# Bidirectional RWKV scan: the group norm's output in its input's memory with four buffers, and inverse blocks placed at the end of a step

## The chip, the cores and the metric

One core of a Trainium2 chip. The metric is the device time of one execution in microseconds, here the median of three runs. Engines are named as in the profile: PE is the matrix engine (PEld its weight loads), DVE the vector engine, ACT the scalar engine, POOL the GpSimd engine, SP the engine whose queue issues nearly all transfers. Every engine works through its own list of instructions in order; an instruction that waits holds up all that stand behind it on that engine.

## The reference, cut to what matters

One trunk layer: SwiGLU, a token mixer, SwiGLU. The change is in the mixer, in the scan over 1152 tokens (128 of context, 1024 latent), in both directions, 16 heads of 64, and in the group norm of what the scan gives:

```python
def _rwkv7_step(S, inp):
    r, w, k, v, kk, a = inp
    sa = jnp.einsum('dbhvk,dbhk->dbhv', S, kk)
    S = S * w[..., None, :] - sa[..., :, None] * (kk * a)[..., None, :] + v[..., :, None] * k[..., None, :]
    return S, jnp.einsum('dbhvk,dbhk->dbhv', S, r)
...
    s_final, y = lax.scan(_rwkv7_step, s0.astype(f32), xs)
    y = _from_scan(y)
    mu = jnp.mean(y, -1, keepdims=True)
    var = jnp.mean(jnp.square(y - mu), -1, keepdims=True)
    y = ((y - mu) * lax.rsqrt(var + GN_EPS)).reshape(b, t, D_A) * p['lnx_g'] + p['lnx_b']
    bonus = jnp.sum(r_h * k_h * p['r_k'], -1, keepdims=True) * v_h
    y = (y + bonus.reshape(b, t, D_A)) * g
```

## The kernel before

The scan runs in chunks of 64 tokens. Two halves of the heads (hb 0 and 1, eight heads each) take 18 steps each, so there are 36 steps; a step handles one chunk of the forward and one of the backward direction, side by side in partitions 0 to 63 and 64 to 127. The order of all five engines is written out by hand in this stage (the `manual_schedule` of L1236); what the next stage issues on ACT, DVE, POOL and SP may be mixed in by a scheduler near the end.

**A step** is `main` (L1085). PE multiplies the states into `xy` (L1104, L1110); ACT copies half of it to `Xs` (L1114); then comes slot 0. PE multiplies `Xs` with the inverse block `W` into `us` (L1120), ACT copies it negated to `vu` (L1123); then comes slot 1. PE forms `sp` (L1130), DVE adds it to the state `Sc` (L1131, L1132), PE finishes `xy` (L1136), ACT copies the outputs to `yt` (L1140). After that the transposes `KBT` (PE L1081, ACT L1083) and, at the end of the step, slot 2. PE's L1081 needs a PSUM buffer that DVE's L1131 has to have read. The three slots are calls of `slot_work` (L1217), each followed by matrix products of the gates as a filler of PE (lines 937 to 941; their weights pass ACT L149 and POOL L150).

**The inverse blocks.** `Solve` (L749) inverts the 64x64 triangles of four steps at once while the four steps before run. Its work is cut into pieces numbered n, and n = 3 x (step - 4 i + 8) + slot, so n % 3 is the slot: loads of `Gq` (n = 0, eight transfers on SP), load of `Wd` (n = 1), `pairs` on DVE (L776, L778; n = 2 to 11), `swap` (two transposes on DVE, L786 and L787; n = 12, slot 0), `back` (four loads of `Nt`, L795), `place` (L802: ACT copies the 32x32 inverses into `Wb`, once for each direction), and `ph1`, `ph2` (L811, L818: 64 small products on PE and two ACT copies each). Four steps have one `swap`: steps 0, 4, 8 and so on.

**The group norm** (L1157) is a generator that advances by one slot at a `yield`. It starts in slot 0, at most one per step; there are 18 of them, and five end after the scan, in a loop (L1268) that advances those left and issues ten filler products each time. A norm loads one direction of `y` from memory (L1163, buffers `y0`, three of them) and takes the other from an SBUF buffer (`y1`) or a second copy; POOL adds them (L1170); DVE takes the mean (L1173), POOL subtracts it (L1176), ACT squares (L1178), DVE sums (L1181), POOL takes the power (L1183) and multiplies (L1185); PE transposes (L1193); ACT scales into `yo` (L1197); POOL adds the bonus term `bb` (L1199); SP stores `yo` to `yn` (L951). `bb` and `yo` have one buffer each:

```python
            yo = gn.tile([P, 4, P], F32, name="yo", tag="yo")
            for k in range(4):
                kt = 4 * hb + k
                A.activation(yo[:, k, :], pt[:, k, :], AF.Identity, bias=pcol("lnx_b", kt), scale=pcol("lnx_g", kt))
            yield
            G.tensor_tensor(yo, yo, bb, ALU.add)
            later(yn_d[hb][tt // 3][:, :, sl], yo)
```

`later` puts a store off to the beginning of the next slot (`flush`). The stage that follows loads `yn` and multiplies it with the projections (L1290 on; its products are lines 158 to 160).

Of the kernel before, what the change touches and what calls it, by code (L numbers as in the profile page):

```python
# [9 lines left out]
F32 = mybir.dt.float32  # L10
# [7 lines left out]
P = 128  # L18
# [43 lines left out]
def tile_step(ctx: ExitStack, tc: tile.TileContext, I: dict, O: dict):  # L62
# [414 lines left out]
    with pool("facc") as facc, pool("f1w", side="right") as wmore, pool("f1p", 6, psum=True) as psum, pool("f1a", 2, psum=True) as paux:  # L477
# [6 lines left out]
        with pool("st") as sp:  # L484
# [36 lines left out]
            with tc.manual_schedule(engines={PE.engine, S.engine}):  # L521
                for kt in range(KT + 1):
                    if kt < KT:
                        mods01(kt)
                    if kt:
                        k = kt - 1
# [70 lines left out]
    with pool("mp", 4, psum=True) as psum, pool("ma", 2, psum=True) as paux, \  # L597
# [151 lines left out]
        class Solve:  # L749
# [75 lines left out]
            def at(self, n):  # L825
                if n == 0:
                    self.loads()
                elif n == 1:
                    self.init()
                elif n < 12:  # L830
                    self.pairs((2, 1, 5)[n % 3])
                elif n == 12:
                    self.swap()
                elif n == 13:
                    self.back()
                    self.place(0)
                elif n == 15:
                    self.place(1)
                elif n == 17:
                    self.ph1(0)  # L840
                elif n == 18:
                    self.ph2(0)
                elif n == 20:
                    self.ph1(1)
                elif n == 21:
                    self.ph2(1)
# [26 lines left out]
        with pool("m2") as pl:  # L873
            sols = [Solve(i) for i in range(9)]
            for k in range(22):
                sols[0].at(k)
# [149 lines left out]
    with pool("s1") as pl, pool("gn") as gn, pool("spa", 2, psum=True) as psA, pool("spx", 1, psum=True) as psX, \  # L1026
# [58 lines left out]
        def main(s):  # L1085
# [52 lines left out]
            for d in range(2):  # L1138
                y0, y1 = YR[d]
                A.copy(eh(yt[y0:y1, m[d]]), xy[y0:y1, :, d])  # L1140
                if s % 2 == 1 and other(cs[d] // 2, d) <= s % 18:
                    yy = direct[hb, cs[d] // 2, d] = gn.tile([P, 8, 64], F32, name="y", tag=f"y{1 if cs[d] > 1 else d}", bufs=3)
                    for k in range(2):
                        later(yy[64 * k:64 * k + 64], yt[y0:y1, k])
                elif s % 2 == 1:
                    later(y_d[d][hb][cs[d] // 2].rearrange("(k t) c -> t k c", k=2), yt[y0:y1].rearrange("p k h v -> p k (h v)"))
# [10 lines left out]
        def group_norm(hb, tt):  # L1157
            y0 = y1 = None
            for d in range(2):
                y = direct.pop((hb, tt, d), None)  # L1160
                if y is None:
                    y0 = gn.tile([P, 8, 64], F32, name="y", tag="y0", bufs=3)
                    S.dma_start(y0, y_d[d][hb][tt].rearrange("t (h v) -> t h v", h=8))  # L1163
                elif y1 is None:
                    y1 = y
                else:
                    y0 = y
            yield
            yield
# [22 lines left out]
            for k in range(4):  # L1192
                PE.transpose(pt[:, k, :], y0[:, 2 * k:2 * k + 2, :].rearrange("p h v -> p (h v)"), ident)  # L1193
            yo = gn.tile([P, 4, P], F32, name="yo", tag="yo")
            for k in range(4):
# [259 lines left out]
```

## Time and profile before

| | |
|---|---|
| median of three runs | 3393.1 us (3387.86 to 3394.22) |
| the profiled execution | 3397.27 us, its span 3395.5 us |
| PE busy | 3209.4 us (95%), 25742 products |
| DVE, ACT, POOL busy | 2007.4, 1185.9, 1306.5 us |
| chain that ended last, by engine | PE 64%, DVE 15%, DMA 8%, issue 5%, POOL 4%, ACT 3% |
| TensorE clock granted, mean | 0.965 |
| scan, from the first L1104 to the last step's end | 1662.9 to about 2253.7 us |

The table says that PE is busy nearly all the time; whether a wait elsewhere costs anything is read from the idle time of PE and from the clock it was granted in that stretch, not from the shares of the other engines. A clock of 1.00 is 2.4 GHz, 0.50 is 1.2 GHz; a stretch with a value between has some of each. The stretch of the scan is where the change lies.

### The profile page before, as it was taken

The numbers are of one execution on the slowest core, as the hardware profiler recorded it, in microseconds if no ns is written. First come the engines' busy times: TensorE is split into PE (matmuls) and PEld (weight loads), VectorE is DVE, ScalarE is ACT, GpSimd is POOL, SyncE is SP. The second block draws the span as 40 slices with busy tenths as digits, with TensorE's granted clock in tenths as the row PEclk, the third lists the DMA queues.
The fourth block names the chain that finished last, engine by engine and source line by source line (L and its number), as shares of the span: only waits on it lengthen the run. The fifth ranks groups of instructions, "written<-read, shape, count | busy, mean of one in ns | idle before, by whom it ended". The sixth has DMA issues, their size and how long they took to land.

```text
span 3395.5 us, 62626 instructions
## 1 busy us (share of the span) xinstructions
PE 3209.4 (95%) x25742; PEld 3049.6 (90%) x25742; DVE 2007.4 (59%) x3300; ACT 1185.9 (35%) x2006; POOL 1306.5 (38%) x1026
## 2 busy tenths in 40 slices
PE   7999999999999999878999889989999999999997
PEld 7999999999897887668888778878999999999996
DVE  6888633346637787875677767545674322223467
ACT  4111111124534454452355555544453111111133
POOL 5111211125546666664321442277762111111144
PEclk9999999999999999879999999989999999999998
DMA  6444211123454555457456566557541111111142
GB/s 235 129 131 144 92 50 38 38 75 131 147 210 146 157 164 162 149 162 238 126 162 188 156 197 213 149 172 238 177 147 38 50 39 40 49 38 48 52 134 97
DMA packets 271534, 433.30 MB, mean 128 GB/s; under 512 B 77840, under 2 KB 173584, under 8 KB 270224
## 3 DMA queue, kind: packets, MB, share of 16 engines
q1 hardware_dynamic: 267792, 424.58, 38.8%
q8 instruction: 202, 3.31, 0.4%
q10 hardware_dynamic: 3456, 4.72, 0.4%
q14 instruction: 84, 0.69, 0.1%
HBM read 311.29 MB, written 96.53 MB: 120 GB/s over the span
## 4 chain that ended last, share of the span: by engine, by line
PE 64%; DVE 15%; DMA 8%; issue 5%; POOL 4%; ACT 3%; SPq 1%; DVEq 0%; POOLq 0%; ACTq 0%
PE pg L159 8%; PE pg L160 8%; PE pg L158 8%; PE po L159 5%; PE po L158 5%; PE po L160 5%; PE pm L158 4%; PE pm L159 4%; PE pm L160 3%; DMA fm<-in_w_mod 2%; DVE fm L403 2%; PE pa L1073 2%; PE xy L1104 2%; DVE wl L127 1%; PE ph L808 1%
## 5 line engine op out<-in xcount | busy, mean ns | idle before, releaser
L125 ACT CAST wh<-wr 128x1024 fp32r<-128x1024 f32 x270 | 280.4, 1048 | 808.7 <-PE po L159 430.2
L127 POOL TENSOR_TENSOR wl<-wr,wh 128x1024 fp32r<-128x1024 f32 x117 | 288.7, 2468 | 496.5 <-ACT wh L125 493.6
L295 POOL TENSOR_TENSOR gl<-sg,gh 128x384 fp32r<-128x384 f32 x132 | 157.8, 1195 | 782.8 <-ACT gh L294 782.8
L159 PE MATMUL pg<-h1l,wh 128*128 128x384 f32 x1056 | 356.9, 338 | 6.8 <-POOL h1l L167 6.8
L158 PE MATMUL po<-gh,wh 128*128 128x384 f32 x1056 | 356.5, 338 | 5.0 <-ACT gh L294 3.0
L159 PE MATMUL po<-gl,wh 128*128 128x384 f32 x1056 | 357.6, 339 | 3.6 <-POOL gl L295 3.6
L158 PE MATMUL pg<-h1h,wh 128*128 128x384 f32 x1056 | 358.1, 339 | 0.0
L160 PE MATMUL pg<-h1h,wl 128*128 128x384 f32 x1056 | 356.1, 337 | 0.0
L160 PE MATMUL po<-gh,wl 128*128 128x384 f32 x1056 | 355.6, 337 | 0.0
L158 PE MATMUL pg<-h3h,wh 128*128 128x384 f32 x1056 | 353.7, 336 | 0.0
L160 PE MATMUL pg<-h3h,wl 128*128 128x384 f32 x1056 | 353.3, 335 | 0.0
L159 PE MATMUL pg<-h3l,wh 128*128 128x384 f32 x1056 | 353.2, 335 | 0.0
L127 DVE TENSOR_TENSOR wl<-wr,wh 128x1024 fp32r<-128x1024 f32 x153 | 222.4, 1458 | 216.2 <-ACT wh L125 216.2
L292 DVE TENSOR_TENSOR sg<-sg,pg 128x384 f32<-128x384 f32 x132 | 73.0, 553 | 459.4 <-PE pg L160 453.3
L158 PE MATMUL pm<-h2h,wh 128*128 128x384 f32 x936 | 326.6, 349 | 3.5 <-ACT pads L442 3.5
L160 PE MATMUL pm<-h2h,wl 128*128 128x384 f32 x936 | 327.6, 350 | 2.2 <-DVE wl L127 2.2
L159 PE MATMUL pm<-h2l,wh 128*128 128x384 f32 x936 | 327.3, 350 | 0.0
L312 DVE SCALAR_TENSOR_TENSOR ac<-po,modh,ac 128x384 f32<-128x384 f32 (+1 forms) x352 | 172.9, 515 | 96.5 <-PE po L160 96.5
L403 DVE SCALAR_TENSOR_TENSOR fm<-fm 128x512 f32<-128x512 f32 x224 | 182.6, 815 | 53.3 <-DMA fm<-in_w_mod 50.3
L159 PEld LDWEIGHTS pg<-h1l,wh 128*128 128x128 f32 x1056 | 200.9, 190 | 9.5 <-POOL h1l L167 8.9
L158 PEld LDWEIGHTS po<-gh,wh 128*128 128x128 f32 x1056 | 199.0, 188 | 7.4 <-ACT gh L294 3.6
L159 PEld LDWEIGHTS po<-gl,wh 128*128 128x128 f32 x1056 | 199.3, 189 | 4.1 <-POOL gl L295 4.1
(287 smaller groups left out, 7466.2 us busy)
## 6 DMA issues: line engine op xcount, KB each, us to landing
wr<-in_ffn_in SPq DMA_DIRECT2D x120, 512.0 KB
ak<-ak SPq DMA_DIRECT2D x48, 768.0 KB
ak<-ak SPq DMA_DIRECT2D x72, 512.0 KB
wr<-in_ffn_out SPq DMA_DIRECT2D x60, 512.0 KB
fm<-in_w_mod SPq DMA_DIRECT2D x112, 256.0 KB
wr<-in_w_mix SPq DMA_DIRECT2D x39, 512.0 KB
sh<-pads SPq DMA_DIRECT2D x108, 130.0 KB
wr<-in_w_mix SPq DMA_DIRECT2D x48, 256.0 KB
```

The costliest lines, as they stand in the source:

```text
L125: A.copy(h[:, :w], r[:, :w])
L127: e.tensor_tensor(l[:, :w], r[:, :w], h[:, :w].bitcast(F32), ALU.subtract)
L158: PE.matmul(ps, wh, xh, start=first and k == 0, stop=False)
L159: PE.matmul(ps, wh, xl, start=False, stop=False)
L160: PE.matmul(ps, wl, xh, start=False, stop=last and k == n - 1)
L292: lastv[0] = V.tensor_tensor(sg, sg, pu[:, :BN], ALU.mult)
L295: G.tensor_tensor(gs[j, b][1][:, sl], sg, gs[j, b][0][:, sl].bitcast(F32), ALU.subtract)
L312: lastv[0] = V.scalar_tensor_tensor(accs[b][:, n, s0:s1], po[:, s0:s1], modh[:, gate_i // 4, n, g:g + 1], accs[b][:, n, s0:s1], ALU.mult, ...
L403: V.scalar_tensor_tensor(jk, w, 1.0, silc[:, s, hf * 512:hf * 512 + 512], ALU.mult, ALU.mult, accum_out=part[:, kt, s, hf:hf + 1])
L808: PE.matmul(pm[o, n % 16, :], x, y, start=True, stop=True)
L1073: PE.matmul(pa[e][:, i, :], ak[es, i, 128:256], ak[es, i, 0:128], start=True, stop=True)
L1104: PE.matmul(xy[:, e, d, i, :], ak[d][es, i, 0:128], states[q, d][es, i, :], start=(i == 0 and d == 0), stop=False, skip_group_check=True)
```

## The change

Three edits. The output of a norm, `yo`, becomes another view of `y0` itself, and `y0` has four buffers instead of three (of the SBUF copies that carry the name `y0`, those of the first chunks in the forward direction, likewise). One of the two `yield`s after the load goes, so that every later part of a norm comes one slot earlier. And of the pieces of `Solve`, `back` and the two `place` move to slot 2 (n = 13 to 14, and 15 to 17), the first `ph1` to slot 0, the two `ph2` to slot 1. Lines after L1167 carry a number lower by one in the kernel after: the add is L1169, the scaling L1196, the last add L1198.

```diff
-                elif n == 13:
+                elif n == 14:
                     self.back()
                     self.place(0)
-                elif n == 15:
+                elif n == 17:
                     self.place(1)
-                elif n == 17:
+                elif n == 18:
                     self.ph1(0)
-                elif n == 18:
+                elif n == 19:
                     self.ph2(0)
                 elif n == 20:
                     self.ph1(1)
-                elif n == 21:
+                elif n == 22:
                     self.ph2(1)
...
-            for k in range(22):
+            for k in range(23):
                 sols[0].at(k)
...
-                    yy = direct[hb, cs[d] // 2, d] = gn.tile([P, 8, 64], F32, name="y", tag=f"y{1 if cs[d] > 1 else d}", bufs=3)
+                    yy = direct[hb, cs[d] // 2, d] = gn.tile([P, 8, 64], F32, name="y", tag=f"y{1 if cs[d] > 1 else d}", bufs=3 + (cs[d] < 2 and d == 0))
...
-                    y0 = gn.tile([P, 8, 64], F32, name="y", tag="y0", bufs=3)
+                    y0 = gn.tile([P, 8, 64], F32, name="y", tag="y0", bufs=4)
                     S.dma_start(y0, y_d[d][hb][tt].rearrange("t (h v) -> t h v", h=8))
                 elif y1 is None:
                     y1 = y
                 else:
                     y0 = y
-            yield
             yield
             G.tensor_tensor(y0, y0, y1, ALU.add)
...
-            yo = gn.tile([P, 4, P], F32, name="yo", tag="yo")
+            yo = y0.rearrange("p (k i) v -> p k (i v)", k=4)
```

How the order moves, at three places. First ACT in step 17 (steps are counted from 0), from the copy `Xs` to the next; L1197 and L1196 scale the norm's output, L802 places an inverse block. Before:

```order
L1114 COPY Xs<-xy 64x2x4x64 x2
L802 COPY Wb_13518<-Yt 32x32x32 x2
L1197 ACTIVATE yo<-pt,par 128x128 x4
L1123 ACTIVATE vu_0_13526<-us 64x512
L1123 ACTIVATE vu_0_13528<-us 64x512
L149 CAST wh<-wr 128x512
L1140 COPY yt<-xy 64x2x4x64 x2
L1083 COPY KBT_19139<-pt 128x512
```

and with the change:

```order
L1114 COPY Xs<-xy 64x2x4x64 x2
L1123 ACTIVATE vu_0_13526<-us 64x512
L1123 ACTIVATE vu_0_13528<-us 64x512
L1177 ACTIVATE y<-y 128x512
L149 CAST wh<-wr 128x512
L1140 COPY yt<-xy 64x2x4x64 x2
L1083 COPY KBT_19136<-pt 128x512
L802 COPY Wb_13518<-Yt 32x32x32 x2
L1196 ACTIVATE y<-pt,par 128x128 x4
```

Between `Xs` and `vu` nothing is left; the placing and the scaling stand behind `yt`, and the square (L1177) has come forward to between `vu` and `yt`.

Second SP in step 20, from the loads for a solve to those of the next step (`Nt` is loaded by `back`, `Wd` holds the identity on which `pairs` start). Before:

```order
L795 DMA Nt<-nd_1_1_177 32x4x128
L795 DMA Nt<-nd_1_1_183 32x4x128
L769 DMA Wd<-in_id 128x1024
L1188 DMA bb<-bon_0_89 128x4x128
L951 DMA yn_2_157<-yo 512x1x128
L140 DMA wr<-in_w_mix 128x512
```

and with the change:

```order
L765 DMA Gq<-qd_1_1_171 16x1x1024 x2
L1187 DMA bb<-bon_0_89 128x4x128
L140 DMA wr<-in_w_mix 128x512
L951 DMA yn_2_157<-y 512x1x128
L769 DMA Wd<-in_id 128x1024
L795 DMA Nt<-nd_1_1_177 32x4x128
L795 DMA Nt<-nd_1_2_184 32x4x128
```

`Wd` now stands ahead of the loads of `Nt` (there are four), and behind `bb` and the store of a norm, which stood behind it.

Third POOL at the end of step 17, up to the clearing of a state (L1041) with which the second half of the heads begins. Before:

```order
L1199 TENSOR_TENSOR yo<-yo,bb 128x512
L1185 TENSOR_TENSOR y<-y,gvr 128x512
L1176 TENSOR_TENSOR y<-y,gmu 128x512
L150 TENSOR_TENSOR wl<-wr,wh 128x512
L1170 TENSOR_TENSOR y<-y 128x512
L150 TENSOR_TENSOR wl<-wr,wh 128x512
L1041 MEMSET Sc_14681 128x256
```

and with the change:

```order
L1198 TENSOR_TENSOR y<-y,bb 128x512
L1184 TENSOR_TENSOR y<-y,gvr 128x512
L1175 TENSOR_TENSOR y<-y,gmu 128x512
L1169 TENSOR_TENSOR y<-y 128x512
L150 TENSOR_TENSOR wl<-wr,wh 128x512
L1182 TENSOR_TENSOR gvr<-gvr,half 128x8
L150 TENSOR_TENSOR wl<-wr,wh 128x512
L1041 MEMSET Sc_14681 128x256
```

The power of the next norm (L1182) has come ahead of the clearing; the three operations on top are now in slot 0 instead of slot 1, and the add of the loaded `y` in slot 1 instead of slot 2.

## Rows read from the trace of the kernel before

**Rows 1.** Windows view, scan: us, PE, PEld, DVE, ACT, POOL busy, clock, DMA, GB/s.
```profile
1680.00:1695.70 15.70, 15.48 (x289) 13.69 (x288) 12.97 (x29) 11.09 (x19) 5.66 (x6) 1.00 0.62 177
...
1929.80:1948.50 18.70, 15.72 (x227) 14.04 (x226) 16.14 (x27) 11.29 (x21) 9.68 (x8) 0.91 0.49 132
1948.50:1975.60 27.10, 16.88 (x293) 15.19 (x291) 15.03 (x33) 11.80 (x21) 12.00 (x11) 0.87 0.65 200
...
2025.00:2048.70 23.70, 18.64 (x293) 16.76 (x292) 14.01 (x34) 11.75 (x21) 10.30 (x9) 0.78 0.59 180
...
2229.80:2253.70 23.90, 23.90 (x398) 21.94 (x398) 10.07 (x18) 11.96 (x24) 16.82 (x14) 1.00 0.43 124
2253.70:2304.30 50.60, 33.17 (x136) 29.71 (x135) 16.13 (x23) 18.30 (x39) 34.23 (x26) 0.73 0.63 198
```

**Rows 2.** Waits view, PE, scan: who waited for whom, total us, times, longest.
```profile
PE pt L1081 <- DVE Sc L1131: 14.3, 10, 3.0
PE sp L1130 <- ACT vu L1123: 12.7, 4, 7.3
...
PE xy L1104 <- POOL Sc L1041: 3.7, 2, 2.2
```

**Rows 3.** Timeline, ACT, steps 17 and 21: start, us, what, idle before.
```profile
1952.94 2.10 ACT L802 COPY Wb<-Yt 32x1024 f32<-32x1024 f32 x2
1962.18 1.51 ACT L1197 ACTIVATE yo<-pt,par 128x128 f32<-128x128 f32 x4 [7.14 <-DMA yn<-yo]
...
2034.96 1.51 ACT L1197 ACTIVATE yo<-pt,par 128x128 f32<-128x128 f32 x4 [3.48 <-DMA yn<-yo]
```

**Rows 4.** Timeline, DVE, steps 16, 17 and 21.
```profile
1941.09 0.67 DVE L1181 TENSOR_REDUCE gvr<-y 128x8 f32<-128x512 f32 x1
...
1959.88 0.20 DVE L776 TENSOR_TENSOR pr<-Wd,Gq 128x31 f32<-128x31 f32 x1 [12.45 <-DMA wr<-in_w_op]
...
1967.83 0.41 DVE L1131 TENSOR_TENSOR Sc<-Sc,sp 128x256 f32<-128x256 f32 x1
...
2033.64 0.19 DVE L776 TENSOR_TENSOR pr<-Wd,Gq 128x31 f32<-128x31 f32 x1 [9.28 <-DMA bb<-bon]
```

**Rows 5.** Timeline, SP's queue, step 20.
```profile
2025.64 2.51 SPq L795 DMA_DIRECT2D Nt<-nd  x4
2028.26 0.52 SPq L769 DMA_DIRECT2D Wd<-in_id  x1
```

**Rows 6.** Waits view, SP, scan.
```profile
SPq L1163 <- PE pt L1193: 15.0, 3, 7.3
```

**Rows 7.** Timeline, POOL, step 17.
```profile
1957.55 1.26 POOL L1170 TENSOR_TENSOR y<-y 128x512 f32<-128x512 f32 x1 [9.20 <-DMA y<-y]
...
1975.24 0.56 POOL L1041 MEMSET Sc<- 128x256 f32 x2
```

**Rows 8.** Chain of waits, step 17: start, us, what.
```profile
1959.90 7.96 DMA y<-y
```

**Rows 9.** Timeline, POOL, after the scan's end.
```profile
2260.14 1.65 POOL L1183 TENSOR_TENSOR gvr<-gvr,half 128x8 f32<-128x8 f32 x1 [6.49 <-DVE gvr L1182]
...
2285.36 1.28 POOL L150 TENSOR_TENSOR wl<-wr,wh 128x512 fp32r<-128x512 f32 x1 [3.67 <-ACT wh L149]
...
2304.96 1.30 POOL L1199 TENSOR_TENSOR yo<-yo,bb 128x512 f32<-128x512 f32 x1 [6.46 <-ACT yo L1197]
```

**Rows 10.** Timeline, ACT, after the scan's end.
```profile
2256.89 0.51 ACT L1306 CAST gh<-gh 128x384 fp32r<-128x384 f32 x1 [7.59 <-DMA gh<-gd_d]
...
2303.32 1.51 ACT L1197 ACTIVATE yo<-pt,par 128x128 f32<-128x128 f32 x4 [9.84 <-DMA yn<-yo]
```

**Rows 11.** Waits view, PE, 2250 to 2320 us.
```profile
PE pm L158 <- ACT yh L166: 2.7, 1, 2.7
```

**Rows 12.** Timeline, DVE, steps 12 and 34: the same operation without and beside POOL.
```profile
1868.86 0.42 DVE L1132 TENSOR_TENSOR Sc<-Sc,PCst 128x256 f32<-128x256 f32 x1
...
2239.03 1.27 DVE L1132 TENSOR_TENSOR Sc<-Sc,PCst 128x256 f32<-128x256 f32 x1
```

## The prediction, made blind

> **What bounds the kernel now.** I read the windows view first, cut at the steps of the scan [rows 1]. An undisturbed step is PE's own work: step 1 takes 15.7 us, PE is busy in 15.48 of them, and its clock is 1.00. Nothing that ACT, DVE, POOL or SP do there costs time. So the change is worth only what it takes from steps that are longer, and from the stretch behind the scan. Three such places stand out. Steps 16 and 17 take 18.7 and 27.1 us, with PE busy for 15.72 and 16.88 and the clock at 0.91 and 0.87: 14.4 us more than two undisturbed steps (18.7 + 27.1 - 2 x 15.7). Step 21 takes 23.7 at a clock of 0.78, 8.0 more than step 1. The stretch from the end of the last step until PE reaches the next stage takes 50.6 us; PE is busy in 33.17 of them, at a clock of 0.73.
>
> The waits view, for PE over the whole scan, says who ends PE's idle time [rows 2]: DVE's read of `sp` (14.3 us in 10 waits), ACT's `vu` (12.7 us in 4), POOL's clearing of the state (3.7 us in 2). ACT is late with `vu` in steps 17 and 21 because the scaling into `yo` stands before it, and that one waits for the store of the last norm's `yo` [rows 3]: 7.14 and 3.48 us idle. One buffer, and a store that comes two slots after the scaling: that is the wait which the change takes away. DVE is late because `pairs` in the first slots of a solve wait for their loads, 12.45 us idle in step 17 and 9.28 in step 21 [rows 4]; of `Gq` and `Wd`, which they read, `Wd` is issued last, behind 2.51 us of `Nt` [rows 5]. And SP itself is held up: in three places, for 15.0 us together, it waits for PE's transposes of a norm, since a load into `y0` needs a buffer that they have read [rows 6].
>
> **The change part by part.** No work is added or removed but a `yield`; what moves is order, and one buffer goes from `yo` to `y0`.
>
> *The scaling no longer waits for a store.* It writes over `y0`, which PE has just read; nothing else is pending. The 7.14 and 3.48 us of ACT go, and the scaling (1.51 us) and the placings move from between `Xs` and `vu` to slot 2. What is late next in step 17 is DVE: its first product of `pairs` starts at 1959.88, and the read of `sp` that PE's next transposes need at 1967.83, 8 us later [rows 4]. `Wd` ahead of `Nt` is issued 2.5 us earlier [rows 5], so this read comes at about 1965.3. The two sums of a norm on DVE (0.67 us each, with a small operation behind each) leave slot 0 for slot 2, which takes another 1.5 us or so out of that queue ahead of the state. Of step 17 that gives 2.5 to 4 us, not 7.3. Behind it stands POOL's clearing at 1975.24 [rows 7]: the load of `y` for step 17 lands about 1967.9 (1959.90 and 7.96 [rows 8]), and the add, two operations on weights and now also the power follow it, 1.3 + 1.3 + 1.65 + 1.3, so that PE can go on at about 1974 instead of 1975.6. I take 6 us for steps 16 and 17 together, of the 14.4: some 4 of step 17, and 2 of step 16, where the sums stood between the transposes of `swap` and the read of `sp`. The lower end is 3, the upper 14, if DVE and POOL also catch up.
>
> *Step 21.* Here both causes shrink: ACT's 3.48 us go, SP's wait for `y0` ahead of `Gq` goes with the fourth buffer, and `Wd` comes 2.5 us earlier. Of the three waits on `y0` (15.0 us, so 5 each [rows 6]) one lies here, so DVE gets `Wd` about 7 us earlier than 2033.64. Nothing of the 8.0 us is left to hold PE; I take 7, at least 4, at most 8.
>
> *Other steps.* The shorter waits for `vu` (of the 12.7 us the longest took 7.3 and most of the rest is step 21's) lie in step 5, where the scaling stands before `vu` as well: 1 us. Of the 14.3 us for DVE some in steps 9 and 25 depend on `Wd` too; I count 2, which makes 3 together, between 0 and 6. The waits behind `swap` (steps 4, 8, 24, 28) stay: `swap` is not moved.
>
> *What is added.* Slot 2 of ACT now holds a placing (2.10 us) and a scaling (1.51 [rows 3]) in the same step where a solve and norms coincide, and the square has left it; `Xs` of the next step stands behind them. Some four steps may start `Xs` half a microsecond late: 2 us lost, 0 to 6. The products of `ph` take a PSUM buffer in slot 1 between `us` and `sp`; ACT reads it in two short copies, covered by the filler of slot 1.
>
> *Behind the scan.* Five norms remain in whole or in part, and their chain is serial: scaling, add, store, next scaling. POOL, which has most of the work (34.23 of 50.6 us busy [rows 1]), idles for 6.49, 3.67 and 6.46 us [rows 9]. The second is a cast of weights behind a waiting scaling on ACT, the third the last scaling, which waited 9.84 us for a store [rows 10]; both go, 10.1 us. The first comes from ACT standing at a cast of the next stage (L1306, 7.59 us [rows 10]), whose place is the same with the change; it stays. The norms being one slot ahead, about one more operation (1.3) lies before the end of the scan. So POOL's last add ends some 11 us earlier, at about 2295, and then POOL bounds this stretch. The next stage needs that last store before its further loads (PE still waits 2.7 us for them after it has started [rows 11]), so the 11 us carry through; behind it PE is busy without breaks to the end, and keeps them. Lower end 4 (the first wait grows), upper 16.
>
> The sum: 6 + 7 + 3 - 2 + 11 = 25 us. The profiled execution took 3397.27 us, 4.2 above the median of 3393.1; taken off the median, 25 us give **3368 us**. All lower ends (3 + 4 + 0 - 6 + 4) give 5 us, so 3388; all upper ends (14 + 8 + 6 - 0 + 16) 44 us, so 3349.
>
> **Weighing a rule.** DVE's update of the state takes 0.42 us where POOL does nothing, and 1.27 where POOL multiplies or subtracts beside it [rows 12]. In the sum I let that pass: the three POOL operations of a norm that move from slot 1 to slot 0 cost DVE in the one slot what they give back in the other. The Trainium skill speaks against that (SBUF — State Buffer, section "Who interferes with whom"): DVE and GpSimd share a port pair, an exclusive lock, and the one that comes second stands still, so what counts is whose operation in slot 0 is on the path. If that decided, the sum would be the 9 us of the second rival instead of 25.
>
> **The rivals.**
>
> *Loads still set the pace (only the stretch behind the scan gains).* For it: in step 17 ACT, DVE and POOL wait for transfers, all from one SP queue, whose order changes little. Against it: `vu` waits for a store which no longer matters. The time: 11 us less, minus 0 to 2: 3383.
>
> *POOL holds up DVE in slot 0.* The three operations take up to 1.3 us each (1.30 for the last add [rows 9]), and DVE's neighbours there are `swap` and, one slot on, the state. If DVE stands still for all three, 3.9 us a step, in the four steps (16, 17, 20, 21) where DVE is late already [rows 4], 16 of the 25 us are lost: 3384. For it: the two durations of [rows 12]. Against it: elsewhere PE hardly waits for DVE.
>
> *The add becomes the bound, slower than before.* The add of the loaded `y` comes one slot earlier, so POOL stands at it with weights for the filler behind it. A load was seen to take 7.96 us [rows 8], and even two slots after its issue the add once waited 9.20 [rows 7]. In the last two steps POOL is busy for 16.82 of 23.90 us [rows 1], so 3.5 us a step are spare; from a wait of more than that in each step, PE waits for what is beyond it. At 7 us a wait in some 14 steps with norms, 3.5 x 14 = 49 us are lost, 25 won: 3417. Against it: the gap is POOL's alone as long as its weights are ahead of the filler.
>
> *Nothing changes.* `y0` is now held until its store has landed, instead of until PE has read it; if the store is as late as it is now, SP waits there as it does for the transposes, and the 15.0 us [rows 6] come back, the clock's losses with them. Then the gain behind the scan is given back in it: 3393.
>
> **How the numbers follow.** The forecast, both parts gain: 0.64. Only behind the scan: 0.14. POOL against DVE: 0.08. The add as bound: 0.07. No change: 0.07. A measurement of this kernel tells 0.2%, 6.8 us, from no change. The forecast, the second and the third case lie below 3386, so faster has 0.86; same 0.07; slower 0.07. The forecast's own ends are 3349 and 3388; they hold the second and third case too. I leave the range at 3346 to 3389.
>
> **What would show it.** Step by step in the new profile: no wait of ACT's scaling for a store of `yn`; PE's waits for `vu` in the scan down from 12.7 to under 3 us; step 21 near 16 us; steps 16 and 17 still over 31 together, with DVE or POOL named; SP no longer waiting at L1163 for PE's transposes; from the scan's last step to the next stage about 40 us instead of 50.6, with POOL the busiest there. POOL against DVE would show as longer DVE operations in slot 0 and as waits of PE at L1081 above 14.3 us. The prediction is wrong if POOL's wait at the add grows to several microseconds a step and PE's filler then waits for POOL, or if SP waits at L1163 for stores.

## The result and the profile after

The kernel with the change takes 3415.61 us (median of seven runs, 3403.12 to 3425.22), the kernel before, timed beside it, 3394.22 (3387.86 to 3402.11). The ratio is 1.005 with a 95% interval of 1.0031 to 1.007: it is slower, by about 17 us going by the ratio (the two medians are 21 us apart), where 25 us of gain were forecast, and it lies outside the range of 3346 to 3389.

The profiled execution of the change took 3403.12 us (span 3401.3, clock 0.967), the fastest of its seven; that of before, 3397.27, was 3 us above its median. So the two traces show 5.8 us of the difference, and they split it plainly. The scan, counted as in the table of before from the first L1104 to the end of the last step, takes 612.5 us instead of 590.8 (**+21.7**). What lies behind it, to the end of the program, takes 1130.8 instead of 1141.8 (**-11.0**). The part ahead of the scan was 4.9 us shorter in this execution; nothing in it is changed, and over the 15 kernels of this study the start of the scan lies anywhere from 1653.2 to 1665.9.

So the gain behind the scan came as large as forecast, and the scan lost twice as much. The windows view of the change, cut at its own steps 14, 16, 17, 18, 20, 21 and at the stretch from the last step to PE's first product of the next stage (columns as in [rows 1]):

```profile
1893.90:1917.40 23.50, 19.57 (x419) 17.22 (x418) 18.07 (x32) 14.24 (x28) 12.31 (x10) 0.93 0.44 127
1934.30:1953.90 19.60, 15.78 (x229) 14.06 (x228) 15.58 (x26) 10.13 (x19) 6.14 (x5) 0.91 0.56 162
1953.90:1981.50 27.60, 15.80 (x227) 14.00 (x226) 20.86 (x43) 10.85 (x19) 14.70 (x13) 0.89 0.60 172
1981.50:2005.50 24.00, 22.81 (x420) 20.80 (x420) 10.43 (x20) 10.44 (x20) 5.98 (x6) 0.77 0.33 101
2020.90:2041.60 20.70, 16.86 (x227) 15.12 (x226) 15.69 (x27) 10.30 (x18) 7.37 (x6) 0.84 0.60 182
2041.60:2062.20 20.60, 16.76 (x227) 15.03 (x226) 16.42 (x35) 10.41 (x18) 7.71 (x6) 0.83 0.61 181
...
2270.50:2307.15 36.65, 25.36 (x128) 23.28 (x127) 10.07 (x20) 17.55 (x39) 32.20 (x26) 0.91 0.58 188
```

The same view of the kernel before, for the steps that [rows 1] left out (14, 18, 20) and for the last stretch, cut like that of the change at the first product of the next stage (1.6 us ahead of where [rows 1] cut it):

```profile
1897.10:1914.50 17.40, 16.22 (x351) 14.47 (x350) 13.67 (x28) 11.89 (x23) 10.99 (x9) 1.00 0.44 138
1975.60:1993.50 17.90, 17.90 (x354) 16.35 (x354) 13.26 (x30) 9.34 (x18) 6.69 (x6) 0.90 0.44 130
2008.80:2025.00 16.20, 14.46 (x229) 12.86 (x228) 15.01 (x27) 9.05 (x16) 6.88 (x6) 1.00 0.65 186
...
2253.70:2302.66 48.96, 31.64 (x128) 28.51 (x127) 15.04 (x21) 17.32 (x36) 34.23 (x26) 0.72 0.64 201
```

Steps 14, 18 and 20, which had no term in the prediction's sum, are 6.0, 6.1 and 4.5 us longer. (Steps 14 and 18 now hold more products of `ph`, 419 and 420 instead of 351 and 354, which left their neighbours: step 13 is 1.6 us shorter, so steps 13 and 14 lose 4.4 together.) Step 21 is 3.1 shorter instead of 7, and step 22, which now holds 64 more products, taken from step 21, is 2.6 longer. In the last stretch the same 128 products keep PE busy for 25.36 us at a clock of 0.91 instead of 31.64 at 0.72; so about half of the 12.3 us there is the clock, and the other half idle time that went.

The waits view of PE over the scan, against [rows 2]:

```profile
PE pt L1081 <- DVE Sc L1131: 28.3, 12, 5.0
PE xy L1104 <- POOL Sc L1041: 7.8, 2, 6.8
PE ph L808 <- issue: 4.5, 4, 1.8
...
PE pw L939 <- POOL us L1003: 2.6, 2, 2.0
```

The wait for `vu` (12.7 us) is gone, as forecast. But the wait for DVE's read of `sp` has doubled, from 14.3 to 28.3, and that for POOL's clearing of the state from 3.7 to 7.8. Of the 14.0 us that the read of `sp` adds, 7.2 lie in steps 17 and 21, where PE had waited for `vu` before, and 4.3 in steps 4, 16 and 20, where it is a loss of its own. Why DVE is late there can be seen in the timeline of DVE in step 20 of the change, from its reading of `pa` to the read of `sp`:

```profile
2025.14 1.29 DVE L1075 TENSOR_TENSOR LM<-pa,sc 128x512 f32<-128x512 f32 x2
2026.35 1.00 DVE L776 TENSOR_TENSOR pr<-Wd,Gq 128x60 f32<-128x60 f32 x1
2027.38 0.97 DVE L778 TENSOR_TENSOR Wd<-Wd,pr 128x60 f32<-128x60 f32 x1
2028.38 0.96 DVE L776 TENSOR_TENSOR pr<-Wd,Gq 128x31 f32<-128x31 f32 x1
2029.38 1.20 DVE L778 TENSOR_TENSOR Wd<-Wd,pr 128x31 f32<-128x31 f32 x1
2030.61 2.03 DVE L786 STREAM_TRANSPOSE Xi<-Wd 128x1024 f32<-128x1024 f32 x1
...
2034.24 0.42 DVE L1131 TENSOR_TENSOR Sc<-Sc,sp 128x256 f32<-128x256 f32 x1
```

and in the timeline of POOL in the same microseconds:

```profile
2025.99 1.28 POOL L1198 TENSOR_TENSOR y<-y,bb 128x512 f32<-128x512 f32 x1
2027.22 1.05 POOL L1184 TENSOR_TENSOR y<-y,gvr 128x512 f32<-128x512 f32 x1
2028.22 1.05 POOL L1175 TENSOR_TENSOR y<-y,gmu 128x512 f32<-128x512 f32 x1
2029.22 1.29 POOL L150 TENSOR_TENSOR wl<-wr,wh 128x512 fp32r<-128x512 f32 x1
```

Before, with POOL idle there, the timeline of DVE had the same four operations in 0.87 us together:

```profile
2012.99 1.29 DVE L1075 TENSOR_TENSOR LM<-pa,sc 128x512 f32<-128x512 f32 x2
2014.19 0.21 DVE L776 TENSOR_TENSOR pr<-Wd,Gq 128x60 f32<-128x60 f32 x1
...
2014.95 0.22 DVE L778 TENSOR_TENSOR Wd<-Wd,pr 128x31 f32<-128x31 f32 x1
...
2020.61 0.42 DVE L1131 TENSOR_TENSOR Sc<-Sc,sp 128x256 f32<-128x256 f32 x1
```

Four small operations of DVE beside four large ones of POOL take 4.13 us, one for one. They stand ahead of `swap` and of the read of `sp`: from the read of `pa` to that of `sp` DVE takes 9.1 us instead of 7.6, although two sums (0.68 us each, with a small operation behind them) have left that stretch. The chain that ended last runs through all four in this step. Over the whole scan, the groups view gives for the pairs and for the update of the state, first before, then with the change (count, busy us, mean ns, idle before):

```profile
L778 DVE TENSOR_TENSOR Wd<-Wd,pr 128x31 f32<-128x31 f32 (+15 forms) x217 | 96.1, 443 | 7.5
L776 DVE TENSOR_TENSOR pr<-Wd,Gq 128x31 f32<-128x31 f32 (+15 forms) x217 | 86.8, 400 | 47.6 <-DMA bb<-bon 13.6 <-DMA wr<-in_w_op 12.4 <-DMA wr<-in_w_mix 5.5
L1132 DVE TENSOR_TENSOR Sc<-Sc,PCst 128x256 f32<-128x256 f32 x71 | 52.7, 742 | 2.4
```

```profile
L778 DVE TENSOR_TENSOR Wd<-Wd,pr 128x31 f32<-128x31 f32 (+15 forms) x217 | 105.7, 487 | 7.4
L776 DVE TENSOR_TENSOR pr<-Wd,Gq 128x31 f32<-128x31 f32 (+15 forms) x217 | 98.5, 454 | 32.7 <-DMA Nt<-nd 16.2 <-DMA wr<-in_w_op 5.0 <-DMA wr<-in_w_mix 4.9
L1132 DVE TENSOR_TENSOR Sc<-Sc,PCst 128x256 f32<-128x256 f32 x71 | 45.9, 646 | 2.4
```

The pairs take 21.3 us more (182.9 to 204.2), the update 6.8 less. That was one thing; two more show on POOL, in steps 14 and 17 of the change:

```profile
1904.48 1.22 POOL L1175 TENSOR_TENSOR y<-y,gmu 128x512 f32<-128x512 f32 x1
1910.42 1.28 POOL L1169 TENSOR_TENSOR y<-y 128x512 f32<-128x512 f32 x1 [4.71 <-DMA y<-y]
...
1978.32 1.65 POOL L1182 TENSOR_TENSOR gvr<-gvr,half 128x8 f32<-128x8 f32 x1 [6.87 <-DVE gvr L1181]
...
1981.14 0.56 POOL L1041 MEMSET Sc<- 128x256 f32 x2
```

The add waits 4.71 us for its load in step 14, with the split of the filler's input (L1003) behind it; and in step 17 the clearing stands behind a norm's power that waited 6.87 us for DVE.

### The profile page after: what moved, and what is told of

Its sections match the earlier page's. It is cut to its first block, busy times and chain, and to the rows that moved or that the text cites. A ratio compares the mean times of both kernels' runs of the same rounds, so it can differ in the third digit from the quotient of the medians.

```text
span 3401.3 us, 62619 instructions
## 1 busy us (share of the span) xinstructions
PE 3206.3 (94%) x25742; PEld 3045.7 (90%) x25742; DVE 2019.3 (59%) x3300; ACT 1187.1 (35%) x2006; POOL 1304.0 (38%) x1026
## 4 chain that ended last, share of the span: by engine, by line
PE 65%; DVE 15%; DMA 7%; issue 4%; POOL 3%; ACT 3%; SPq 1%; DVEq 0%; POOLq 0%; ACTq 0%
PE pg L159 9%; PE pg L160 9%; PE pg L158 9%; PE po L159 5%; PE po L158 5%; PE po L160 5%; PE pm L158 4%; PE pm L159 4%; PE pm L160 4%; PE pa L1073 2%; PE xy L1104 2%; DMA fm<-in_w_mod 2%; DVE wl L127 1%; DVE fm L403 1%; DVE Wd L778 1%
## 5 line engine op out<-in xcount | busy, mean ns | idle before, releaser
L403 DVE SCALAR_TENSOR_TENSOR fm<-fm 128x512 f32<-128x512 f32 x224 | 182.3, 814 | 52.4 <-DMA fm<-in_w_mod 49.1
L294 ACT CAST gh<-sg 128x384 fp32r<-128x384 f32 x132 | 67.5, 511 | 385.9 <-DVE sg L292 385.9
```

The lines of the kernel that those rows point to most:

```text
L294: A.copy(gs[j, b][0][:, sl], sg)
L403: V.scalar_tensor_tensor(jk, w, 1.0, silc[:, s, hf * 512:hf * 512 + 512], ALU.mult, ALU.mult, accum_out=part[:, kt, s, hf:hf + 1])
```

## The experiments

All ratios are against the kernel before on the same chip, with 95% intervals. Lengths of steps and of the scan are read from one trace of each kernel; step 0 takes 14 us in five of the traces and 17 in ten, whichever edits they have, so two scans that differ by 3 us are not told apart. Lines of `yo` and of the norm keep the numbers of the kernel that each is made from, give or take one.

**Which of the three edits.** Four kernels with a part of the change each. (The buffer without the earlier norm wasn't tried: `y0` would then be held until a store that SP issues behind the next load into `y0`.)

Moved inverse blocks alone:
```diff
-                elif n == 13:
+                elif n == 14:
                     self.back()
                     self.place(0)
-                elif n == 15:
+                elif n == 17:
                     self.place(1)
...
```


> The kernel before with the moved inverse blocks alone (place, back and the products of ph a slot or two later; both yields, yo and three buffers kept). Theory A, the norms are the cause (one slot earlier, POOL's subtraction, multiplication and last add run in slot 0 beside DVE's pairs and the reads of pa, and the read of sp comes late): this edit alone is no change, ratio 0.998 to 1.002, DVE's read of sp ends about 14 us of PE's idle time as before. Theory B, the moved blocks are the cause (a product of ph stands in the same step as its neighbour, and ph in slot 0 or 1 takes the PSUM buffer that us or sp wants): the scan gets longer by 15 to 22 us, ratio 1.004 to 1.007. Theory C, the buffer is the cause (y0 held until its store landed): no change, as under A.

Measured: 1.0014 (1.0006 to 1.0023), 3398.5 us; PE's wait for the read of `sp` 15.4 us. A small cost, not the 0.5%.

One yield less, alone:
```diff
-            yield
             yield
             G.tensor_tensor(y0, y0, y1, ALU.add)
```


> The kernel before with one yield less ahead of the add, nothing else. Theory A: the scan is 15 to 30 us longer and only a part of the gain behind it comes (the norms are one slot ahead, but the scaling still waits for a store): ratio 1.004 to 1.008, DVE's read of sp ends 25 us or more of PE's idle time. Theory B: no loss in the scan, a few us gained behind it, 0.997 to 1.000. Theory C: as under B.

Measured: 1.0043 (1.0031 to 1.0055), 3409.8 us; the scan 611.9 us, the wait for the read of `sp` 33.0 us, steps 4, 16 and 20 together 58.9 us (before: 50.8). This edit alone gives the loss.

The yield and the buffer, without the moved blocks:

> The change without the moved inverse blocks: one yield less, yo in y0, four buffers. Theory A: as the change or near it, ratio 1.002 to 1.007, with 25 us or more of PE's idle time ended by DVE's read of sp. Theory B: the scan is back at 591 us or shorter and the 11 us behind it stay, 0.993 to 0.998. Theory C: as the change, 1.003 to 1.007, with SP waiting at L1163 for stores.

Measured: 1.0046 (1.0033 to 1.0059); scan 606.1 us, wait for the read of `sp` 34.0.

The yield and the moved blocks, without the buffer:

> The change without the buffer: one yield less and the moved inverse blocks, yo kept, three buffers. Theory A: slower than before by more than the change, since the scaling waits for the store again: ratio 1.005 to 1.010. Theory B: as the change without the gain behind the scan, 1.006 to 1.009. Theory C: scan as before, 0.998 to 1.001.

Measured: 1.0056 (1.0039 to 1.0072); scan 612.2 us.

Theory A stands, B and C fall: every kernel with the yield taken out lies at 1.0043 to 1.0056, whatever else it has, and the buffer makes no difference that these intervals show. Two things fell out of the same traces. With the yield alone, three buffers and `yo` in its own place, PE's waits for `vu` in the scan are 0.6 us, and SP no longer waits at L1163 for PE's transposes: both were credited to the buffer, and both go by the order alone. And the stretch from the scan's end to the program's end is 1133.6 us with the yield alone, against 1141.8.

**What of the earlier norm.** Two theories: A1, the three large POOL operations in slot 0 stretch DVE's pairs; A2, the add waits for its load one slot earlier and holds POOL up.

The yield taken out elsewhere (one of the two ahead of the transposes), the rest of the change kept:
```diff
+            yield
             yield
             G.tensor_tensor(y0, y0, y1, ALU.add)
...
             S.dma_start(bb, bon_d[hb][tt // 3][:, :, sl])
             yield
-            yield
```


> The change with the yield ahead of the add put back and one of the two ahead of the norm's transposes taken out in its place: add, subtraction and multiplication stand in their old slots (2, 1, 1), transposes and scaling in slot 2, the last add alone in slot 0. Theory A1 (POOL's three large operations in slot 0 stretch DVE's pairs and swap there): only one of the three is left in slot 0, so DVE's pairs lose most of their 21 us of extra length, the scan returns to about 590 us and the 8 to 11 us behind it stay: ratio 0.995 to 0.999. Theory A2 (the add that waits for its load one slot early holds POOL up, 63.7 us idle in front of it against 27.9): the same numbers, since the add is back too; the next kernel tells the two apart. Against both: if the scaling in slot 2 is what delays, 1.003 or more.

Measured: 0.9989 (0.9978 to 1.0), 3390.2 us; scan 597.7 us, 14.8 less than with the change, though not at 590; behind the scan 1128.7; pairs 190.6. PE's waits for the read of `sp` still sum to 26.0 us, 9.3 of them in step 17, where the wait for `vu` has gone; step 21 takes 16.3 us. The late place has a price too: step 4 takes 20.1 us (15.9 before), where the norm's transposes on PE now wait 1.4 us for POOL's multiplication and the clock is 0.83.

The add early, all else of the norm in its old slots (from the kernel before):
```diff
-            yield
             yield
             G.tensor_tensor(y0, y0, y1, ALU.add)
...
+            yield
             yield
             G.tensor_tensor(y0, y0, mu.unsqueeze(2).broadcast_to([P, 8, 64]), ALU.subtract)
```


> The kernel before with one yield moved from ahead of the add to behind the sums: the add alone comes a slot earlier and waits for its load as in the change; subtraction, multiplication and last add stay in slot 1, away from slot 0. Theory A1: no change, 0.998 to 1.002, and DVE's pairs last as long as before (183 us for all L776 and L778 of the scan). Theory A2: the scan is 15 to 25 us longer, 1.003 to 1.007.

Measured: 1.0034 (1.002 to 1.0048), 3405.0 us; the scan is 601.0, 10.2 us longer and so less than A2 expected; the pairs last 188.6 us, and the wait for the read of `sp` is 14.3 as before. So A2 holds too, by its ratio, but in its own place: step 14 takes 25.5 us (17.5 before), step 17 31.2 (27.1). The waits view of PE in its scan shows who is late there, and the timeline of POOL in step 14 why:

```profile
PE pw L939 <- POOL us L1003: 6.8, 2, 6.4
PE pm L941 <- POOL wl L150: 5.9, 1, 5.9
```

```profile
1909.66 1.26 POOL L1169 TENSOR_TENSOR y<-y 128x512 f32<-128x512 f32 x1 [6.51 <-DMA y<-y]
1910.88 1.15 POOL L167 TENSOR_TENSOR u<-uf,u 128x384 fp32r<-128x384 f32 x1
1911.99 1.14 POOL L1003 TENSOR_TENSOR us<-uf,us 128x384 fp32r<-128x384 f32 x1
```

POOL stands 6.51 us at the add, and what PE's filler needs stands behind it in the queue.

The change with the three POOL operations cut to an eighth:
```diff
-            G.tensor_tensor(y0, y0, mu.unsqueeze(2).broadcast_to([P, 8, 64]), ALU.subtract)
+            G.tensor_tensor(y0[:, 0:1], y0[:, 0:1], mu[:, 0:1].unsqueeze(2).broadcast_to([P, 1, 64]), ALU.subtract)
...
```


> The change with POOL's subtraction, multiplication and last add cut to the first head of eight (the other heads' columns are left out of these three), all waits, loads and the order as in the change. Theory A1: the stretching in slot 0 goes, L776 and L778 together from 204 us to 185 or less, DVE's read of sp ends 14 us or less of PE's idle time instead of 28.3, the scan is 590 us or less: ratio 0.992 to 0.997. Theory A2: the add still waits for its load, the scan stays at 605 to 612 us: 0.999 to 1.004.

Measured: 0.9993 (0.9983 to 1.0003); pairs 189.5 us, scan 604.5, wait for the read of `sp` 25.6. The ratio is A2's, and so is the scan but for half a microsecond, the pairs nearer to A1's 185, and the wait misses A1's 14 by far: 10.1 us of it are in steps 17 and 21, which the cut doesn't shorten (8.8 us with full operations). By steps the two theories come apart: steps 4, 16 and 20 fall from 59.5 us together to 49.1 (before: 50.8), and step 14 stays at 23.5. The timelines of DVE and of POOL in its step 20 show the mechanism once more:

```profile
2024.06 0.21 DVE L776 TENSOR_TENSOR pr<-Wd,Gq 128x60 f32<-128x60 f32 x1
2024.31 0.22 DVE L778 TENSOR_TENSOR Wd<-Wd,pr 128x60 f32<-128x60 f32 x1
2024.57 1.27 DVE L776 TENSOR_TENSOR pr<-Wd,Gq 128x31 f32<-128x31 f32 x1
```

```profile
2023.67 0.29 POOL L1175 TENSOR_TENSOR y<-y,gmu 128x64 f32<-128x64 f32 x1
2024.49 1.27 POOL L150 TENSOR_TENSOR wl<-wr,wh 128x512 fp32r<-128x512 f32 x1 [0.53 <-ACT wh L149]
```

The small operations end before the pairs begin and the first two last 0.21 and 0.22 us; the third meets the weights' L150 of 1.27 us and lasts 1.27 itself.

The control, the same cut in the kernel before:

> The kernel before with the same three POOL operations cut to the first head: the control. Theory A1: here they meet the update of the state in slot 1 (L1132, 52.7 us in the scan), which falls to some 35 us, with DVE's pairs unchanged near 183; PE's idle time ended by DVE falls from 14.3 to about 10, and POOL's work behind the scan shrinks: 0.994 to 0.998. Theory A2: 0.997 to 1.000, from the stretch behind the scan alone.

Measured: 0.9975 (0.9964 to 0.9987); pairs 175.5 us, L1132 48.5 instead of the 35 expected: most of what stretches the update is not the norm's three operations. Wait for the read of `sp` 14.1, where 10 were expected, scan 589.0. With small operations the change costs 0.9993 / 0.9975, some 0.2%, against 0.5% with full ones.

**The clearing.** The two states of the second half are free once the first two steps and the store of their result have read them.
```diff
             for d in range(2):
-                G.memset(states[0, d], 0.0)
+                if hb == 0:
+                    G.memset(states[0, d], 0.0)
                 S.dma_start(states[1, d], I["state"][d][:, 4 * hb:4 * hb + 4])
...
+                if s == 8:
+                    for d in range(2):
+                        G.memset(states[0, d], 0.0)
```
In the kernel before:

> The kernel before with the clearing of the two states of the second half issued in step 8 instead of ahead of step 18 (nothing reads or writes them in between; the load of the other two stays). Theory K, the clearing stands in POOL's queue behind the norm and is a term of its own: PE's wait of 2.2 us ahead of step 18 goes, steps 17 and 18 together (45.0 us) get 2 to 3 us shorter: ratio 0.998 to 1.000. Rival L, the next thing is as late (the load of the other state, or DVE's update in step 17): no change and a wait of PE at the same line for a load.

Measured: 0.9994 (0.9984 to 1.0004), no difference in the time; the wait is gone, and steps 17 and 18 take 41.0 us instead of 45.0 in its trace.

In the change:

> The change with the clearing issued in step 8. Theory K: the 6.8 us of PE's wait ahead of step 18 go, and the low clock that followed (11.2 us in step 18) shrinks to about 3: steps 17 and 18 together from 51.6 to 38 to 45 us: ratio 1.001 to 1.003 against 1.005 for the change. Rival L: 1.004 to 1.006.

Measured: 1.0025 (1.0012 to 1.0038), 3402.9 us. Theory K: half of the loss against before. Its windows of steps 17 and 18:

```profile
1956.80:1978.00 21.20, 16.45 (x229) 14.73 (x228) 16.25 (x35) 9.92 (x17) 11.46 (x9) 0.84 0.66 192
1978.00:1996.40 18.40, 17.77 (x421) 16.15 (x420) 15.97 (x27) 11.05 (x21) 9.29 (x7) 1.00 0.55 160
```

39.6 us instead of 51.6: the 6.8 us of idle PE are gone and step 18 runs its 421 products at a clock of 1.00 instead of 0.77. (Other steps of this trace happen to be 7 us longer, so that its scan, 607.7, shows only part of it; the medians decide.)

**Together.** Late yield and early clearing, with all else of the change:

> The late yield and the early clearing together, with the buffer and the moved inverse blocks. Theory K: 1.7 us of the wait for the clearing go and some of the low clock of step 18 (48.6 us for steps 17 and 18 there, 43 to 46 here): ratio 0.996 to 0.9985, faster than before. Rival L: 0.998 to 1.000.

Measured: 0.9987 (0.9975 to 1.0), 3388.4 us. The median is L's, the interval holds both. Steps 17 and 18 take 44.8 us instead of 48.6 in the traces, but the time of the whole hardly differs from that of the late yield alone (0.9989): where the clearing is only a little late, moving it gives too little to be told from nothing.

The same with the inverse blocks where they were:

> As the kernel with late yield and early clearing, but with the inverse blocks where they were. Moving them alone cost a ratio of 1.0014, most of it behind step 17 (step 18: 17.9 to 22.0 us) and in steps 22 and 30 (2.5 and 1.9 us). If that adds up here: 0.994 to 0.997. If the blocks only paid in step 18 because the clearing stood there (rival): as the kernel with them, 0.996 to 0.9985.

Measured: **0.9962 (0.995 to 0.9974), 3380.4 us: faster than both kernels.** The moved blocks cost here as well. Steps 22 and 30 are 1.8 and 2.6 us shorter without them than with them, or 1.3 and 1.2 with the steps ahead of them, whose products they take over. Where the rest of the difference lies the two traces don't show: they took 3382.0 us with the moved blocks and 3384.9 without, the other way round than the medians.

And this one without the buffer:

> The kernel before with two edits only: the yield taken out ahead of the norm's transposes instead of the add, and the clearing issued in step 8; yo in its own memory, three buffers, inverse blocks as before. It differs from the fastest kernel so far (ratio 0.9962) by the buffer alone. If the buffer is worth what the prediction gave it (the scaling's waits for a store of 7 and 3.5 us in the scan and most of the 11 us behind it): 0.999 to 1.001. If the gain behind the scan comes from the norms being a slot ahead, and the buffer is worth nothing (rival): 0.9955 to 0.997, with the stretch behind the scan at 1134 to 1138 us as in the kernel with the yield alone.

Measured: 0.9976 (0.9965 to 0.9986), 3382.3 us, between the two expectations; the stretch behind the scan 1136.0 us against 1132.4. The intervals overlap, so that the buffer's worth is some 0.1%, not settled by this pair alone. In step 17 of this trace the scaling waits 10.43 us for a store, and PE 8.1 us for the `Xs` behind it; with the buffer both waits are gone, and PE waits 10.1 us for the read of `sp` instead: the step takes 27.9 us without the buffer and 29.7 with it. Step 21, for which the prediction counted on the buffer, takes 17.3 without it and 16.8 with it. Behind the scan all traces with one slot less say the same: with the buffer 1128.7 to 1134.6 (six kernels without cut operations, mean 1131.6), without it 1133.6 to 1136.0 (three, mean 1134.6), with both yields 1140.3 to 1141.8 (before, moved blocks alone, add early, before with early clearing).

## Why the prediction was wrong

**The step that failed** is a sentence: that the three POOL operations which move from slot 1 to slot 0 "cost DVE in the one slot what they give back in the other". With the change the pairs take 21.3 us more and the update 6.8 less. Not all of this is the doing of the three: cut to an eighth, they still leave the pairs at 189.5 us in the change, against 175.5 in the kernel before, so their size is worth 14.7 us of the pairs in the change and 7.4 in the kernel before. Of the time it is worth some 0.3%, the difference between what the change costs with full and with small operations. The balance is uneven because the price goes by DVE's operations, not by POOL's time: in slot 1 two updates of 0.42 us meet POOL [rows 12], in slot 0 the four operations of two pairs, the last of them 0.2 us each, and each waits out a POOL operation of its own. The rival with this mechanism had 0.08; it priced 3.9 us of POOL in steps 16, 17, 20 and 21, all of it as gain lost. In fact steps 4, 16 and 20 became longer than before (50.8 to 59.5 us), and step 4 had been counted as unchanged.

The rule of the Trainium skill that was weighed (SBUF — State Buffer, "Who interferes with whom") and not followed was the better guide: that the trace agrees is shown by 0.21 us against 1.27 for the same operation, with POOL between jobs and beside one. The time worked out for that case, 3384, was 32 us short all the same.

**Term by term.**

- Steps 16 and 17, 6 us gained: they take 47.2 instead of 45.8 together. The wait for `vu` went; DVE and POOL were late next, as the text said, but later than it said: PE goes on at 1981.5 in place of the forecast 1974. There the clearing was in the sum, with "now also the power" ahead of it at 1.65 us, as if that could start at once; it waited 6.87 for DVE. The low clock in step 18 (0.77) came on top and stood in no term. With the clearing out of the way, steps 17 and 18 are 12 us shorter. While the clearing is late, the moved blocks have a part in it: alone, with every norm as before, they make these two steps 49.6 us instead of 45.0, since step 17 gets no shorter without 64 of its products (27.6), and step 18, which runs them, has a clock of 0.77 instead of 0.90:

```profile
1971.60:1993.60 22.00, 22.00 (x418) 20.10 (x418) 13.42 (x30) 10.63 (x20) 6.87 (x7) 0.77 0.50 150
```

- Step 21, 7 us: 3.1, and 0.5 with step 22, since the moved blocks only shift products from the one to the other (alone: 2.4 shorter and 2.5 longer). ACT and SP no longer hold it up; PE waits 3.8 us for the read of `sp`. The forecast gain comes with the yield taken out later: 6.9 us in the fastest kernel, and 6.4 without the buffer, so by the order and not by the buffer.
- Steps 13 and 14, no term: 4.4 us lost together, by the add that waits for its load (with the add early and nothing else, step 14 alone lost 8.1). The rival *The add becomes the bound* named this wait and the filler behind it. Its time, 3417, is close to the median of 3415.6, but by accident: it counted 3.5 us in 14 steps, and it was one step that paid (in the trace of the add early, two), since elsewhere the weights were ahead.
- Slot 2 of ACT and the moved blocks, 2 us lost: the moved blocks alone cost 0.14%, or 4.7 us, in their trace mostly in steps 17 and 18.
- Behind the scan, 11 us: 11.0 in the trace. The amount was right, the reason mostly not. It was put down to the scaling's waits for a store (10.1 us) with 1.3 for the norms being a slot ahead. The runs turn it round: the slot gives 6.5 us (the means 1141.1 and 1134.6), the buffer some 3 more (1134.6 and 1131.6, from ranges that overlap). With the yield alone the last scalings still wait 5.53 and 4.07 us for stores, and yet the stretch is nearly as short:

```profile
2304.51 1.50 ACT L1196 ACTIVATE yo<-pt,par 128x128 f32<-128x128 f32 x4 [5.53 <-DMA yn<-yo]
...
2313.66 1.51 ACT L1196 ACTIVATE yo<-pt,par 128x128 f32<-128x128 f32 x4 [4.07 <-DMA yn<-yo]
```

POOL's timeline of the change answers to [rows 9]: 4.32 us at the first power instead of 6.49, and 0.74 and 1.20 in place of 3.67 and 6.46, so POOL is the busiest there (32.20 of 36.65 us). That it alone bounds the stretch is not shown: of the chain that ended last between 2270 and 2310 us, transfers are 43%.

```profile
2272.47 1.65 POOL L1182 TENSOR_TENSOR gvr<-gvr,half 128x8 f32<-128x8 f32 x1 [4.32 <-DVE gvr L1181]
...
2303.36 1.30 POOL L150 TENSOR_TENSOR wl<-wr,wh 128x512 fp32r<-128x512 f32 x1 [0.74 <-ACT wh L149]
...
2309.45 1.27 POOL L1198 TENSOR_TENSOR y<-y,bb 128x512 f32<-128x512 f32 x1 [1.20 <-DMA bb<-bon]
```

The sum in the trace, with steps taken together where the moved blocks shift products from one to the next: +8.7 (steps 4, 16, 20: the pairs) + 4.4 (steps 13 and 14: the add) + 6.6 (steps 17 and 18: the late clearing, the clock behind it and the moved blocks) + 1.8 (steps 29 and 30: the moved blocks, which cost 0.5 there alone) - 0.5 (steps 21 and 22) + 0.7 elsewhere = 21.7 us. The causes named are those that the experiments bear out for these steps; the shares within 6.6 us were not taken apart.

**What stays open.** The change's median lies 12 us above its profiled execution; which steps are longer in the other runs no trace shows. In the fastest kernel one wait of 10.1 us for the read of `sp` is left in step 17; DVE's pairs ahead of it had stood 13.33 us for a load, so that what the first rival named may be next there; no run tests it. A norm's last add still meets pairs in slot 0; a solve's last pairs in another slot were not tried. Which of the moved pieces costs the 0.14% was not taken apart.

## What to carry to other kernels

When a generator that feeds several engines loses a slot, every later part moves, so write down for each large POOL operation which DVE operations it now stands beside, and count those with both inputs in SBUF: each may cost a whole POOL operation, however small it is. Take the slot out late in the chain, where fewer parts move (here 14.8 us of scan between two places for the same edit), and look at what then waits for the part ahead of it. Products moved out of a step that waits may leave it as long as it was (step 17 here) and lengthen the step that takes them. And an operation that is needed once at a fixed step, like a clearing, belongs in the queue as early as its data allow, not behind a chain that may wait.

## What was not expected of the hardware

DVE's share of the loss depends on what the operation reads. Pairs with both inputs in SBUF went from 0.21 to 1.27 us beside a POOL operation of 1.27 us; the update L1132, both inputs in SBUF, from 0.42 to 1.27 [rows 12]. The reads of PSUM beside POOL did not change: in step 17 of the change L1131 takes 0.41 us inside one of POOL's operations on weights, and the L1132 behind it 1.05; all 72 of L1131 take 29.8 us before and 30.0 with the change, and `swap`'s transposes (one input) stay near 2 us (in step 20 the first took 2.18 us before, and 2.03 with POOL's add beside it). The Trainium skill (SBUF — State Buffer, "Who interferes with whom") says that a DVE instruction with two SBUF inputs contends with a GpSimd instruction that reads SBUF, which these durations bear out. That the two engines then take turns, one short operation of DVE for one long one of POOL, is what made four operations of 0.2 us into 4.13 us.

A step with hardly any idle PE can carry the cost of the one before it: in step 18 of the change PE waits for 1.2 us in all and has a granted clock of 0.77 (11.2 us at 1.2 GHz, the rest at 2.4), behind a wait of 6.8 us that ended where the step begins. With 4.8 us of idle time in step 17 instead of 11.8, step 18 had 1.00. But where the wait ends counts too: in the fastest kernel PE stands 10.1 us in step 17, the wait ends inside that step, and the low clock falls there (0.72), while step 18 has 0.99:

```profile
1948.70:1978.40 29.70, 19.62 (x291) 17.61 (x290) 15.95 (x39) 11.17 (x20) 11.19 (x9) 0.72 0.62 192
1978.40:1994.90 16.50, 16.50 (x355) 15.01 (x354) 11.17 (x24) 9.22 (x18) 6.94 (x6) 0.99 0.38 113
```
